# A hybrid trunk step: all eight gates of the attention's output branch computed among the independent linears

## The chip, the cores and the metric

The kernel runs on one core of a Trainium2 chip. The metric is the device time of one execution in microseconds (us); lower is better. TensorE (PE) multiplies, VectorE (DVE) and ScalarE (ACT) work elementwise, GpSimd (POOL) has little to do here, and SyncE (SP) issues nearly all DMA transfers, in the order of its queue.

## What is computed

A trunk of two layers works on 640 tokens of width 1024: 128 prompt tokens and 512 sample tokens. In each layer one wide projection feeds three branches, a gated short convolution, a bidirectional gated DeltaNet and an attention, and each branch has its own gate of 1024 columns:

```python
h = rms_norm(x, lp['g_pre1']) * (1 + sc1) + sh1
(cb, cc, cx, aq, ak, av, dn_q, dn_k, dn_v, dn_z, dn_beta, dn_a, gate_logits) = jnp.split(
    h @ lp['w_in'], SPLIT_IDX, axis=-1)
ya = (cb * depthwise_conv(cc * cx, lp['conv_w'])) @ lp['w_pa']
yb = block_attention(q, keys, vals) @ lp['w_pb']
yc = gated_deltanet_bidir(dn_q, dn_k, dn_v, dn_z, ...) @ lp['w_pc']
ga, gb, gc = jnp.split(jax.nn.sigmoid(gate_logits), 3, axis=-1)
mix = (ga * ya + gb * yb + gc * yc) @ lp['w_o']
x = x + gt1 * rms_norm(mix, lp['g_post1'])
h2 = rms_norm(x, lp['g_pre2']) * (1 + sc2) + sh2
ffn = (silu(h2 @ lp['w_gate']) * (h2 @ lp['w_up'])) @ lp['w_down']
```

The shifts, scales and gates of the modulation (`sh1`, `sc1`, `gt1` and so on) come from products of a conditioning vector with `w_mod`.

## The kernel before

Activations stand transposed, as eight tiles of 128 columns by 640 tokens, and are worked on in two halves of 320 tokens. Each fp32 product is made of three products in a shorter format: a tile is split into a high and a low part (ScalarE's cast `whi` at L94, VectorE's difference `wlo` at L95), and `mm3` multiplies high by high, high by low and low by high (L363 to L365). A **linear** is 128 output columns: 8 tiles of the contraction, two halves, three products, 48 matmuls, with two weight loads of 256 KB (`wraw`). The halves of a linear alternate by four tiles (12 matmuls), and each fills one of three PSUM banks (`NL` = 3, L72), so the second half of a linear can start only when the first half of the linear before it has been copied out.

The DeltaNet works on four heads in two pairs (`delta_pair`). For each head the projections k, q and v are computed and convolved (`dn_qkv`, `dn_post`, whose padded copy is `padc` at L861 and whose result is `dz`), turned over by TensorE (`nat`, L899), multiplied with themselves (`kk`, L946) and scaled by decays. The decays of a head are read back from DRAM, spread over the partitions (`rowb`, L905), and ScalarE exponentiates them first at L960 (`egl`). Then a triangular inverse of 32-wide blocks begins with VectorE's transposes `RA` and `RB` (L998) and TensorE's small products from L1018 on, followed by a scan over five chunks in both directions (`scan`, L1067 to L1079), whose start state `ss` comes from DRAM. The first head of a layer is special: its three projections are part of the group of linears that opens the layer (`lead`), so no linear is issued for them in `delta_pair` (the item is `None`). After both pairs come the keys and values and the attention's heads and stages (`attn_head`), with products `sco`, `psc`, transposes `ptT` (L770) and products with the values `po` (L780 to L782).

All these chains have waits in them. Beside them the kernel puts independent linears: `run(main, fill)` walks through the main chain, whose steps yield a cost in us, and after each step takes steps from the filler until the filler's costs have caught up:

```python
for c in main:
    tm += c * rate
    while fill is not None and tf < tm:
        ...
        tf += t
```

The costs are the constants `Y_*` at the head of the file: `Y_QKV` for a projection or its convolution, `Y_INV` for a step of the inverse (eight per pair, sixteen per layer), `Y_SCAN` for a step of the scan (five per pair, ten per layer). A gate linear yields 6.5. The filler of a layer is

```python
yield from branch(l, 0, ya, "w_pa", True)
yield from gates(l, 2)
yield from gates(l, 1, 0, NGB)
while len(yf) < 4:
    yield None
yield from weave(branch(l, 2, resplit(yf, "F"), "w_pc"), mods, PB)
```

preceded by the output gates of the DeltaNet (`dn_z`) and the convolution branch. `gates(l, b, m0, m1)` computes gate linears of branch b early and stores each result to DRAM (`sgd`, 320 KB); `branch(l, b, ...)` reads those back (`sgl`) and computes the rest at its own place. Branch 1, the attention's, runs after the attention, outside `run`. `mods` are the modulation products of layer 0 for later (`mod_part`, loads `wm` of 512 KB at L317, three buffers, products `pm` at L324): one step is taken per `PB` = 8 us of yields in branches 2 and 1, and the rest at once behind branch 1. In layer 1 there are none. The Tile framework then orders each engine's instructions by its own priorities within these limits.

Of the kernel before, what the change touches and what calls it, by code (L numbers as in the profile page):

```python
# [35 lines left out]
KEEP = ("C", "C", "C", "C", "E", None)  # L36
LEAD = ("C", "C", "C", "C", "E")
F1 = 14
NGB = 4
NPD = 2  # L40
NLD = 2

# [1 line left out]
NSQ = (2, 2, 2, 2, 2, 2, 2, 1)  # L44
ENDG = (3, 7)

Y_QKV, Y_NAT, Y_EL, Y_INV, Y_SCAN, Y_O = 1.127, 4.215, 1.207, 1.962, 2.959, 2.917
Y_AT, Y_AQ, Y_AK, Y_AKK, Y_DO = 0.446, 1.037, 0.438, 2.07, 2.558
PB, PF = 8.0, 11.5

# [2 lines left out]
def tile_trunk(ctx: ExitStack, tc: tile.TileContext, I: dict, O: list, layers=DEPTH):  # L53
# [340 lines left out]
    def linear(src, acts, ev):  # L394


        pb = {}
        i0 = 0
        for hi, lo, nk in wblocks(src, len(acts)):
            for h in range(2):  # L400
                if i0 == 0:
                    pb[h] = lbank()[:, :HF]
                for j in range(nk):
                    ah, al = acts[i0 + j]
                    mm3(pb[h], hi[:, j, :], lo[:, j, :], hv(ah, h), hv(al, h), i0 + j == 0, i0 + j == len(acts) - 1)
                if i0 + nk == len(acts):
                    ev(h, pb[h])
            i0 += nk
# [111 lines left out]
    def gates(l, b, m0=0, m1=KD):  # L520

        for m in range(m0, m1):
            SY.dma_start(out=sgd[b, m], in_=gate(l, b, m))
            gated.add((l, b, m))
            yield 6.5
# [339 lines left out]
    def dn_post(l, which, h, t):  # L865
        y = cslot("dy", (P, 641))
        ci = 92 + which * 4 + h
        conv3(y, t, lambda i: cols[l][:, ci + 12 * i:ci + 12 * i + 1])
        s = cslot("ds", (P, 641))
        A.activation(s, y, AF.Exp, scale=-1.0)  # L870
        sig_tail(s)
        z = cslot("dz")
        V.tensor_mul(z[:, 0:P], y[:, 0:P], s[:, 0:P])
        V.tensor_mul(z[:, P:NT], y[:, P + 1:641], s[:, P + 1:641])
        if which == 0:
            sq = cslot("dsq")
            A.activation(sq, z, AF.Square)

            def later():
                pr = bank("dqr")  # L880
                for c in range(5):
                    T.matmul(pr[:, 2 * c:2 * c + 2], lhsT=sq[:, c * P:(c + 1) * P], rhs=onesc, start=True, stop=True)
                r = rqs[l, h] = small("dqr", (P, 10), 4)
                rstd(r, pr[:, 0:10], 1.0, post=lnq)

            rqs[l, h] = later
        return z
# [20 lines left out]
    def delta_pair(l, hp, gz, out, first=None):  # L908
# [6 lines left out]
        for h in hs:  # L915
# [5 lines left out]
            for w, (item, t) in todo:  # L921
                if item is not None:
                    linear(*item[:3])
                    yield Y_QKV
                res[w] = dn_post(l, w, h, t)
                yield Y_QKV
            kT[h], qT[h] = res[1], res[0]
            Gbs = [rowb(l, 4 * d + h) for d in range(2)]
            kn[h] = nat(kT[h], f"kn{h}")
# [341 lines left out]
    for l in range(layers):  # L1271
# [7 lines left out]
        def mainc():  # L1279
            for hp in range(2):  # L1280
                yield from delta_pair(l, hp, gz, on, qkv if hp == 0 else None)
                for h in (2 * hp, 2 * hp + 1):
                    yf.append(dn_out(l, h, on[h], zs[h]))
                    yield Y_DO
            yield from attn_kv(l, kv)
            yield from attn_q(l, 0, kv, qs)
            pend = []
            for h in range(NH):
                stages, of = attn_head(l, h, kv, qs)
                for n, (fa, fb, pr2) in enumerate(stages):  # L1290
                    args = () if pr2 is None else (pr2,)
                    sm_ = fa(*args)
                    yield Y_AT
                    pend.append((fb, args, sm_))
                    if len(pend) > NPD:
                        f_, a_, s_ = pend.pop(0)
                        f_(*a_, s_)
                        yield Y_AT
                    if n == 0 and h + 1 < NH:
                        yield from attn_q(l, h + 1, kv, qs)  # L1300
                o.append(of)
            for f_, a_, s_ in pend:
                f_(*a_, s_)

        def fillc():
# [6 lines left out]
# [3 lines that stand above are left out]
# [98 lines left out]
```

## Time and profile before

| | us |
|---|---|
| median of 3 runs | 2776.02 |
| lowest and highest run | 2770.52, 2776.62 |
| the profiled execution | 2778.18 |
| its span in the trace | 2776.1 |

The profile is of one execution, 2.16 us above the median; 2.1 us of it lie outside the span. TensorE is busy 98% of the span, at a mean granted clock of 0.991 of full speed. A busy TensorE in these rows may be a matmul that is only queued in the pipeline, so the distance between the starts of matmuls, not the duration of one, tells what a matmul costs in a dense stretch. Layer 0 lies from about 30 to 1400 us and layer 1 from there on.

### The profile page before, as it was taken

What the parts mean: (1) busy time and instruction counts of PE and PEld (TensorE: products, weight loads), DVE (VectorE), ACT (ScalarE), POOL (GpSimd) and SP (SyncE); (2) the same over time, 40 slices, a digit from 0 to 9 for tenths busy, and PEclk for the clock granted to TensorE, in tenths of its full rate; (3) what the DMA queues carried; (4) which work ended last, traced back from release to release, by engine and by line L of the source; (5) the groups of instructions that cost most, each with busy time, mean ns of one, the idle gap of its engine ahead of it and who ended that gap; (6) DMA issues with size and microseconds to landing.
All of it is one profiled execution on the core that took longest, in us unless ns stands there. A gap on an engine that the chain in (4) does not pass through costs nothing.

```text
span 2776.1 us, 49612 instructions
## 1 busy us (share of the span) xinstructions
PE 2709.4 (98%) x19706; PEld 2583.2 (93%) x19706; DVE 1565.0 (56%) x3385; ACT 1256.8 (45%) x2863; POOL 26.5 (1%) x147
## 2 busy tenths in 40 slices
PE   7999999999999999999999999999999999999998
PEld 3899999999898999999978999999999999999997
DVE  4586576477743744224475865754777466442344
ACT  4533554466533633223455335545655354332333
POOL 0000000000000000000000000000000000000001
PEclk9999999999999999999999999999999999999999
DMA  8452355433564344444532323433233432222231
GB/s 240 72 80 48 80 94 112 83 66 96 161 163 154 123 130 152 125 158 145 170 89 58 73 52 82 96 90 85 68 95 117 125 99 88 76 69 76 81 117 62
DMA packets 387512, 288.15 MB, mean 104 GB/s; under 512 B 18667, under 2 KB 348113, under 8 KB 387281
## 3 DMA queue, kind: packets, MB, share of 16 engines
q1 hardware_dynamic: 387280, 285.00, 39.2%
q8 instruction: 154, 2.52, 0.4%
q14 instruction: 78, 0.63, 0.1%
HBM read 251.86 MB, written 33.07 MB: 103 GB/s over the span
## 4 chain that ended last, share of the span: by engine, by line
PE 84%; DVE 7%; DMA 5%; ACT 3%; issue 1%; SPq 0%; ACTq 0%; DVEq 0%
PE l L363 23%; PE l L364 23%; PE l L365 22%; DMA wm<-in_w_mod_dram 2%; PE pm L324 1%; DMA wraw<-in_w_in_dram 1%; PE ptT L770 1%; DMA rowb<-gd 1%; PE po L780 1%; PE scan L1071 1%; PE po L782 1%; PE kk L946 1%; PE sco L363 1%; PE po L781 1%; DVE Tt L990 1%
## 5 line engine op out<-in xcount | busy, mean ns | idle before, releaser
L94 ACT CAST whi<-wraw 128x512 fp32r<-128x512 f32 (+1 forms) x540 | 332.2, 616 | 829.4 <-PE l L364 783.7
L95 DVE TENSOR_TENSOR wlo<-wraw,whi 128x512 fp32r<-128x512 f32 (+1 forms) x540 | 367.4, 682 | 529.5 <-ACT whi L94 513.4
L363 PE MATMUL l<-hh,whi 128*128 128x320 f32 x1856 | 589.0, 317 | 2.8 <-ACT padc L861 2.8
L364 PE MATMUL l<-hl,whi 128*128 128x320 f32 x1856 | 582.7, 314 | 0.0
L365 PE MATMUL l<-hh,wlo 128*128 128x320 f32 x1856 | 581.7, 313 | 0.0
L363 PE MATMUL l<-h2h,whi 128*128 128x320 f32 x1248 | 387.4, 310 | 0.0
L364 PE MATMUL l<-h2l,whi 128*128 128x320 f32 x1248 | 385.3, 309 | 0.0
L365 PE MATMUL l<-h2h,wlo 128*128 128x320 f32 x1248 | 385.3, 309 | 0.0
L363 PEld LDWEIGHTS l<-hh,whi 128*128 128x128 f32 x1856 | 352.0, 190 | 6.5 <-ACT padc L861 3.3
L364 PEld LDWEIGHTS l<-hl,whi 128*128 128x128 f32 x1856 | 351.9, 190 | 2.0
L365 PEld LDWEIGHTS l<-hh,wlo 128*128 128x128 f32 x1856 | 352.1, 190 | 1.0
L363 PEld LDWEIGHTS l<-h2h,whi 128*128 128x128 f32 x1248 | 234.6, 188 | 7.0 <-ACT fs L427 3.1
L364 PEld LDWEIGHTS l<-h2l,whi 128*128 128x128 f32 x1248 | 234.6, 188 | 0.0
L365 PEld LDWEIGHTS l<-h2h,wlo 128*128 128x128 f32 x1248 | 234.6, 188 | 0.0
L363 PE MATMUL l<-ah,whi 128*128 128x320 f32 x544 | 168.8, 310 | 0.0
L364 PE MATMUL l<-al,whi 128*128 128x320 f32 x544 | 168.2, 309 | 0.0
L365 PE MATMUL l<-ah,wlo 128*128 128x320 f32 x544 | 167.9, 309 | 0.0
L363 PE MATMUL l<-rsh,whi 128*128 128x320 f32 x384 | 119.8, 315 | 0.0
L364 PE MATMUL l<-rsl,whi 128*128 128x320 f32 x384 | 118.4, 312 | 0.0
L365 PE MATMUL l<-rsh,wlo 128*128 128x320 f32 x384 | 118.2, 310 | 0.0
L363 PEld LDWEIGHTS l<-ah,whi 128*128 128x128 f32 x544 | 102.2, 188 | 2.2 <-issue 1.3
L365 PEld LDWEIGHTS l<-ah,wlo 128*128 128x128 f32 x544 | 102.2, 188 | 0.0
(427 smaller groups left out, 5328.2 us busy)
## 6 DMA issues: line engine op xcount, KB each, us to landing
wraw<-in_w_in_dram SPq DMA_DIRECT2D x256, 256.0 KB
wm<-in_w_mod_dram SPq DMA_DIRECT2D x80, 512.0 KB
wraw<-in_w_gate_dram SPq DMA_DIRECT2D x88, 256.0 KB
wraw<-in_w_up_dram SPq DMA_DIRECT2D x88, 256.0 KB
wraw<-in_w_down_dram SPq DMA_DIRECT2D x80, 256.0 KB
mixo<-mixd SPq DMA_DIRECT2D x32, 320.0 KB
wm<-in_w_mod_dram SPq DMA_DIRECT2D x32, 256.0 KB
wraw<-in_w_pb_dram SPq DMA_DIRECT2D x32, 256.0 KB
```

The source lines that it names most:

```text
L94: A.copy(hi, src)
L95: V.tensor_sub(lo, src, hi.bitcast(F32))
L324: T.matmul(pm[32 * u:32 * u + 2, 0:256], lhsT=sc[:, k, :], rhs=w[:, u * 256:(u + 1) * 256], start=(n == 0), stop=(n == KD - 1))
L363: T.matmul(out, lhsT=wh, rhs=ah, start=first, stop=False)
L364: T.matmul(out, lhsT=wh, rhs=al, start=False, stop=False)
L365: T.matmul(out, lhsT=wl, rhs=ah, start=False, stop=last)
L770: T.transpose(pt[:, i, q * P:(q + 1) * P], sm_[q][:, kt * P:(kt + 1) * P], ident)
L780: T.matmul(po, lhsT=vh, rhs=th, start=(kt == 0), stop=False)
L781: T.matmul(po, lhsT=vl, rhs=th, start=False, stop=False)
L782: T.matmul(po, lhsT=vh, rhs=tl, start=False, stop=(kt == 4))
L946: chunked("kk", lambda o, c: T.matmul(o, lhsT=kT[h][:, c * P:(c + 1) * P], rhs=rhs[:, c * P:(c + 1) * P], start=True, stop=True), lambda b ...
L990: V.tensor_add(Tt[:, j + 1:32, 0:j], Tt[:, j + 1:32, 0:j], tv)
```

## The change

`NGB` goes from 4 to 8: all eight gates of branch 1 are computed by the filler, stored and read back, and none is left behind the attention. The costs that the main chain yields grow: `Y_INV` from 1.962 to 2.6, `Y_SCAN` from 2.959 to 3.4, and the three convolution steps of the first head of each layer yield a new `Y_FIRST` of 3.5 instead of 1.127. So the filler gets further ahead at these places. No instruction of the linears is added or removed; per layer four gate results more are stored to DRAM and read back.

```diff
--- before.py
+++ after.py
@@ -36,7 +36,7 @@
 KEEP = ("C", "C", "C", "C", "E", None)
 LEAD = ("C", "C", "C", "C", "E")
 F1 = 14
-NGB = 4
+NGB = 8
 NPD = 2
 NLD = 2
 
@@ -44,7 +44,8 @@
 NSQ = (2, 2, 2, 2, 2, 2, 2, 1)
 ENDG = (3, 7)
 
-Y_QKV, Y_NAT, Y_EL, Y_INV, Y_SCAN, Y_O = 1.127, 4.215, 1.207, 1.962, 2.959, 2.917
+Y_QKV, Y_NAT, Y_EL, Y_INV, Y_SCAN, Y_O = 1.127, 4.215, 1.207, 2.6, 3.4, 2.917
+Y_FIRST = 3.5
 Y_AT, Y_AQ, Y_AK, Y_AKK, Y_DO = 0.446, 1.037, 0.438, 2.07, 2.558
 PB, PF = 8.0, 11.5
 
@@ -923,7 +924,7 @@
                     linear(*item[:3])
                     yield Y_QKV
                 res[w] = dn_post(l, w, h, t)
-                yield Y_QKV
+                yield Y_QKV if item is not None else Y_FIRST
             kT[h], qT[h] = res[1], res[0]
             Gbs = [rowb(l, 4 * d + h) for d in range(2)]
             kn[h] = nat(kT[h], f"kn{h}")
```

Line numbers from L49 on are one higher after the change. The change moves instructions as follows.

**First place: TensorE at the first head's products `kk` in layer 1.** `nat` and `kk` belong to the first head, the tiles `l_...` to linears beside them (`hh0` to `hh7` are the eight tiles of the contraction, so a linear's half runs from `hh0` to `hh7`). Before:

```order
L899 MATMUL nat_16237<-ident_64,dz_16219 128x128 x2
L899 MATMUL nat_16242<-ident_64,dz_16219 128x128 x2
L946 MATMUL kk_16333<-dz_16194 128x128 x3
L946 MATMUL kk_16338<-dz_16194 128x128 x2
L946 MATMUL kk_16342<-dz_16206,dz_16194 128x128 x3
L946 MATMUL kk_16347<-dz_16206,dz_16194 128x128 x2
L882 MATMUL dqr_16351<-onesc_67,dsq_16209 128x2 x5
L363 MATMUL l_16417<-hh4_15045,whi_16413 128x320
```

And now:

```order
L365 MATMUL l_16355<-hl7_15064,whi_16338 128x320
L366 MATMUL l_16355<-hh7_15063,wlo_16339 128x320
L947 MATMUL kk_16410<-dz_16206 128x128 x3
L947 MATMUL kk_16415<-dz_16206 128x128 x2
L947 MATMUL kk_16419<-dz_16218,dz_16206 128x128 x3
L947 MATMUL kk_16424<-dz_16218,dz_16206 128x128 x2
L883 MATMUL dqr_16428<-onesc_67,dsq_16221 128x2 x5
L364 MATMUL l_16497<-hh0_15049,whi_16487 128x320
```

Before, `kk` stood in the middle of the second head's first projection, between its tiles 3 and 4. Now the two `nat` rows stand further ahead (out of the piece), and `kk` stands between a finished linear and tile 0 of a linear of the convolution branch; that whole linear of 48 matmuls follows before the second head's next projection.

**Second place: ScalarE at the second head of layer 1.** `egl` waits for the decays, `padc` copies out the second head's projections, `whi` are casts of weights. Before:

```order
L447 COPY ccs_16404<-l_16430 128x320
L94 CAST whi_16565<-wraw_16563 128x512
L960 ACTIVATE egl_16927<-rowb_16784 128x5
L94 CAST whi_16641<-wraw_16639 128x512
L965 ACTIVATE Dt_16382<-Dt_16382 128x640
L861 COPY padc_16469<-l_16493 128x128
L861 COPY padc_16469<-l_16493 128x192
L960 ACTIVATE egl_16949<-rowb_16786 128x5
L94 CAST whi_16647<-wraw_16645 128x512
L861 COPY padc_16469<-l_16506 128x320
```

And now:

```order
L95 CAST whi_16644<-wraw_16642 128x512
L961 ACTIVATE egl_17004<-rowb_16866 128x5
L966 ACTIVATE Dt_16459<-Dt_16459 128x640
L95 CAST whi_16650<-wraw_16648 128x512
L961 ACTIVATE egl_17026<-rowb_16868 128x5
L95 CAST whi_16710<-wraw_16708 128x512
L862 COPY padc_16554<-l_16578 128x128
L862 COPY padc_16554<-l_16578 128x192
L95 CAST whi_16716<-wraw_16714 128x512
L862 COPY padc_16554<-l_16591 128x320
```

Before, the second `egl` stood between the copies of the first and the second half of the first projection; now both `egl` stand ahead of all copies, with one cast more between the last `egl` and the first copy.

**Third place: SyncE's queue at the end of layer 0's mixing, where the modulation loads `wm` stand among the loads of `w_o`.** Before:

```order
L359 DMA wraw<-in_w_o_dram 128x4x128
L490 DMA h2h_9880<-xd 128x640
L490 DMA h2h_9882<-xd 128x640
L490 DMA h2h_9884<-xd 128x640
L359 DMA wraw<-in_w_o_dram 128x4x128
L490 DMA h2h_9886<-xd 128x640
L317 DMA wm<-in_w_mod_dram 128x1024 x3
L359 DMA wraw<-in_w_o_dram 128x4x128
L317 DMA wm<-in_w_mod_dram 128x1024 x2
L359 DMA wraw<-in_w_o_dram 128x4x128 x5
```

And now:

```order
L360 DMA wraw<-in_w_pb_dram 128x4x128
L318 DMA wm<-in_w_mod_dram 128x1024 x2
L360 DMA wraw<-in_w_o_dram 128x4x128 x4
L318 DMA wm<-in_w_mod_dram 128x1024 x2
L360 DMA wraw<-in_w_o_dram 128x4x128 x2
L318 DMA wm<-in_w_mod_dram 128x1024 x2
L360 DMA wraw<-in_w_o_dram 128x4x128
L318 DMA wm<-in_w_mod_dram 128x1024 x7
L360 DMA wraw<-in_w_o_dram 128x4x128 x5
```

Before, the last five loads stood as three and two with the reload of `h2h` ahead of them. Now thirteen stand in this piece, seven of them in a row, and the `h2h` loads stand further ahead in the queue.

## Rows read from the trace of the kernel before

**Rows 1.** The page: the chain that ended last, shares of the span by engine.
```profile
PE 84%; DVE 7%; DMA 5%; ACT 3%; issue 1%; SPq 0%; ACTq 0%; DVEq 0%
```

**Rows 2.** The timeline of TensorE (start, duration, line, operation, tiles, idle before).
```profile
108.06 2.40 PE L946 MATMUL kk<-dz 128*128 128x128 f32 x20
...
1488.71 2.40 PE L946 MATMUL kk<-dz 128*128 128x128 f32 x20
...
1491.98 0.40 PE L363 MATMUL l<-hh,whi 128*128 128x320 f32 x1
...
1492.52 0.31 PE L363 MATMUL l<-hh,whi 128*128 128x320 f32 x1
...
1496.05 0.31 PE L363 MATMUL l<-hh,whi 128*128 128x320 f32 x1
...
1514.66 0.64 PE L363 MATMUL l<-hh,whi 128*128 128x320 f32 x1 [2.52 <-ACT padc L861]
```

**Rows 3.** Busy time by window: PE, PEld, DVE, ACT, POOL, granted clock, DMA, GB/s.
```profile
85.00:110.00 25.00, 21.63 (x155) 21.36 (x154) 12.13 (x20) 14.60 (x34) 0.00 (x0) 1.00 0.27 53
205.00:213.00 8.00, 6.72 (x70) 5.77 (x68) 5.78 (x10) 1.94 (x5) 0.42 (x1) 0.86 0.23 36
213.00:266.00 53.00, 53.00 (x539) 48.14 (x540) 35.66 (x86) 16.27 (x36) 0.00 (x0) 0.96 0.26 49
733.00:760.00 27.00, 23.65 (x192) 18.56 (x191) 20.09 (x55) 15.68 (x45) 0.00 (x0) 1.00 0.62 195
845.00:872.00 27.00, 24.22 (x201) 21.09 (x201) 5.61 (x11) 6.75 (x16) 0.00 (x0) 1.00 0.58 198
1480.00:1517.00 37.00, 32.90 (x222) 31.93 (x221) 23.61 (x50) 20.09 (x57) 1.77 (x16) 0.97 0.29 70
1588.00:1596.00 8.00, 6.76 (x67) 5.80 (x66) 5.70 (x10) 1.94 (x5) 0.42 (x1) 0.82 0.22 39
1844.00:1851.00 7.00, 7.00 (x70) 6.09 (x67) 3.82 (x8) 2.24 (x5) 0.00 (x0) 0.76 0.25 84
2119.00:2136.00 17.00, 14.23 (x95) 11.50 (x94) 13.78 (x41) 11.35 (x34) 0.00 (x0) 1.00 0.15 54
```

**Rows 4.** What TensorE waited for in 1480:1517 (total, times, longest us).
```profile
PE l L363 <- ACT padc L861: 2.8, 2, 2.5
PE nat L899 <- DVE dz L873: 1.3, 1, 1.3
```

**Rows 5.** The timeline of ScalarE in 1490:1516, second head of layer 1.
```profile
1506.82 0.21 ACT L960 ACTIVATE egl<-rowb 128x5 f32<-128x5 f32 x1 [2.04 <-DMA rowb<-gd]
...
1512.10 0.74 ACT L870 ACTIVATE ds<-dy 128x641 f32<-128x641 f32 x1 [3.71 <-DVE dy L566]
```

**Rows 6.** The timeline of ScalarE in 108:132, second head of layer 0.
```profile
124.98 0.21 ACT L960 ACTIVATE egl<-rowb 128x5 f32<-128x5 f32 x1 [3.32 <-DMA rowb<-gd]
...
125.60 0.48 ACT L861 COPY padc<-l 128x128 f32<-128x128 f32 x2
```

**Rows 7.** What TensorE waited for in 200:215, where the first inverse begins.
```profile
PE pw L1018 <- DVE RB L998: 1.3, 1, 1.3
```

**Rows 8.** What TensorE waited for in 470:476, the second pair's scan in layer 0.
```profile
PE scan L1067 <- DMA ss<-in_state_dn_dram: 0.9, 1, 0.9
```

**Rows 9.** What TensorE waited for in 2119:2136, the end of layer 1's attention.
```profile
PE po L780 <- ACT pTh L94: 1.2, 1, 1.2
PE psc L363 <- ACT p L725: 1.1, 1, 1.1
```

**Rows 10.** The timeline of TensorE in 845:872, the modulation products.
```profile
859.72 1.48 PE L324 MATMUL pm<-wm,sc 128*2 128x256 f32 x24 [1.81 <-DMA wm<-in_w_mod_dram]
...
866.48 1.04 PE L324 MATMUL pm<-wm,sc 128*2 128x256 f32 x16 [0.97 <-DMA wm<-in_w_mod_dram]
```

**Rows 11.** The timeline of SyncE's queue in 765:872, the modulation loads.
```profile
851.17 1.28 SPq L317 DMA_DIRECT2D wm<-in_w_mod_dram  x3
...
860.40 1.51 SPq L317 DMA_DIRECT2D wm<-in_w_mod_dram  x2
```

## The prediction

> **What bounds the kernel now.** I read the page first: TensorE holds 84% of the chain that ended last [rows 1], and the change takes no matmul away. So the time can only come from the places where TensorE waits or is clocked down, and the second view is busy time by window around them [rows 3]. The price of a linear comes from the timeline: from 1492.52 to 1496.05 there are 24 starts [rows 2], 0.147 us each, so a linear of 48 matmuls takes 7.05 us. The reader is to see four kinds of loss. In the first head of layer 1 TensorE idles 37 - 32.90 = 4.1 us in the window 1480:1517, and the waits there name ScalarE's `padc` (2.8) and VectorE's `dz` (1.3) [rows 3, 4]. At the start of the first pair's inverse it waits 1.3 us for `RB` [rows 7], and the granted clock is 0.86 in 205:213 and 0.96 in 213:266; layer 1 shows 0.82 at the same place [rows 3]. At the end of each attention it idles 3.35 us (733:760) and 2.77 us (2119:2136). At the end of layer 0's mixing it idles 2.78 us [rows 3], all for `wm` (1.81 and 0.97) [rows 10]. Inside the inverse (213:266) TensorE is busy throughout [rows 3], so a linear that is put there fills nothing.
>
> **The change, part by part.** Four more gates are 4 x 6.5 = 26 of filler cost per layer. Against them the spending grows by 3 x (3.5 - 1.127) = 7.1 at the first head, 16 x (2.6 - 1.962) = 10.2 at the inverse and 10 x (3.4 - 2.959) = 4.4 at the scan, 21.7 in all. The rest, 4.3 or 0.66 of a gate linear, is filler that reaches further into the attention. The matmuls are the same, so I sum up waits.
>
> First head of layer 1. Before, `kk` started at 1488.71 [rows 2]; the queue then held half a linear, a linear and 12 matmuls before the half that needs the bank of the first `padc` copy. That is 3.27 us (`kk` and the small products behind it, to 1491.98 [rows 2]) + 84 x 0.147 = 15.6 us after `kk`, while ScalarE stood at `egl` for `rowb`, the last time until 1506.82, and later until 1512.10 for `dy` [rows 5]. Now a whole linear stands where half a one did, and the need comes at 3.27 + 108 x 0.147 = 19.1 us. ScalarE, with its second `egl` at 18.1 us after `kk` if `rowb` lands as late, has a cast and two copies to go, until about 19.4: 0.3 us of wait are left. The next need, 7.05 later at 26.5, meets a copy that before let TensorE go on at 1514.66, 25.95 us after `kk` [rows 2]. Layer 0 already has this spacing: `kk` at 108.06, the last `egl` at 124.98 and the copy at 125.60, 17.5 us after `kk` [rows 2, 6], where no `padc` wait followed. So -2.8 + 0.3 = **-2.5**. The `dz` wait shrinks by the six matmuls that now stand ahead of it: 6 x 0.147 = **-0.9**. The clock of 0.97 over 37 us is 1.1 us of loss [rows 3]; I take half, **-0.5**, since the waits go but not the small products. Bounds for the three together: -5.2 (all goes) and +1.5 (`rowb` lands later behind more queue traffic).
>
> First head of layer 0: TensorE's 3.37 us in 85:110 are the wait for `dz` behind a blocked ScalarE, whose order is unchanged: **0**, bounds -1.5 and +1.5. Here 3.37 us of idling left the clock at 1.00 [rows 3]. The Trainium skill (TensorE: Matmul & The Clock Gate, Part 1: The HAM clock gate) says that the throttled rate is the default and activity releases it; by that rule alone every wait taken away would return clock too, about another -1 here. The row does not agree, and the sum stays by the row.
>
> Start of the inverse, both layers: seven linears lie between the second `kk` and `RB` before and after, and VectorE's work there is the same list, so `RB` comes as late: **0**. Bounds: -1.3 and -3.2 each (0.14 x 8 + 0.04 x 53 for the clock), +1. Second pair: a clock of 0.76 over 7 us in 1844:1851 [rows 3] is 1.7 us, of which more linears among the small products may return half: **-0.8** (0 to -1.7). Layer 0's scan waits 0.9 us for `ss` [rows 8]; three linears more stand ahead of it, **-0.6** (0 to -0.9).
>
> Ends of the attention. In layer 1, by the order, the filler ended with about 1.3 heads of the attention still to come, and the waits are short ones for `p` and `pTh` [rows 9]; the order now puts linears among them to the end: of 2.77, **-2.5** (0 to -2.8). In layer 0 linears of branch 2 already stood there, and of 3.35 part is `wm`: **-1.2** (+1 to -3).
>
> End of layer 0's mixing. Branch 1 now yields 51.2 us of cost instead of 77.2, so at one step per 8 us 6 of the modulation steps are taken there instead of 9. Counted in TensorE's order, the last groups of products are 12, 12 and 8 as before, but two groups of 8 that stood among branch linears stand now directly ahead of them. A round of three loads went from 851.17 to 860.40, 9.2 us; a round of two from there to the end of its products at 866.48 + 1.04, 7.1 us [rows 10, 11]. Rounds of 2, 3, 3, 2 are 32.6 us; between them lie 2.46 linears (17.3) and 5.0 of products. So up to 10.3, less about 1 by which the same count for the two rounds of before exceeds its 2.8, is exposed: +6.5 over before at most, 0 if the third buffer keeps one load ahead each time. I take **+3.5**. The stores and reloads of four gates more per layer cost nothing in TensorE's time as long as they land before their linear; DMA share is 0.58 to 0.62 in the windows of layer 0 where they fall [rows 3], and if that cover went, it would show as the same kind of wait.
>
> Sum: -2.5 - 0.9 - 0.5 - 0.8 - 0.6 - 2.5 - 1.2 + 3.5 = -5.5. Against the profiled execution 2778.18 gives 2772.7; it stands 2.2 above the median, so the median should go from 2776.02 to **2770.5**.
>
> **The rivals.**
> *Nothing comes out.* The `rowb` landing decides ScalarE, and more DMA traffic could move it by the 3.5 us that the linear wins; then the first head keeps its 3.9, and the attention's 3.7 pays for the modulation's 3.5. Left: -0.8 - 0.6 - 0.2 = -1.6, 2774.4. For it: ScalarE's order keeps both `egl` ahead, now even ahead of all copies. Against: layer 0 [rows 6]. A form of it, that the change does not do what it says, is ruled out by the order: 3.6 instead of 3.3 linears stand inside layer 0's first inverse, 3.5 instead of 2.7 inside the second.
> *Slower: the modulation loads block `w_o`.* Seven `wm` stand in a row in SyncE's queue with `w_o`'s loads behind them. If the rounds are fully exposed (+6.5) and the next weights then land a round late (8.5 us, 851.17 to 859.72), the sum is -5.5 - 3.5 + 6.5 + 8.5 = +6.0, 2782. It decides once the last `wm` is issued later than 1.2 linears (8.5 us) before TensorE reaches the weights behind it; the order gives 1.6 linears, which speaks against it.
> *Faster: the clock holds at the inverse.* If denser linears end the drop at both first inverses early, -6.4 more, 2764. Against: both waits for `RB` stay. The skill's rule that activity releases the throttle (same page and part) is for it; rows 3 show the drop only beside the short products, not at every wait.
>
> **How the numbers follow.** A difference of 0.2%, 5.5 us, is about what a measurement of this kernel can tell from none. Forecast 0.42, with a range of its own of 2765 to 2776 (0.24 faster, 0.17 same, 0.01 slower, as it sits on the mark); nothing 0.32 (0.05, 0.24, 0.03); blocked loads 0.14 (0, 0.02, 0.12); clock 0.12 (all faster). Together faster 0.41, same 0.43, slower 0.16. The range reaches to the rivals at either side, a little past the clock's: 2762 to 2782, with 0.1 left out on each side.
>
> **What would show it.** Right: in layer 1's second head no `padc` wait over 1 us; the wait for `RB` and the clock at 205:213 and 1588:1596 as before; linears up to the end of layer 1's attention with under 0.5 us idle; and `wm` waits of 4 to 8 us at the end of layer 0's mixing. Wrong: `wm` waits over 10 us or a wait for `w_o` weights, `padc` still waiting over 2 us, or a granted clock near 1.00 at the inverse.

## The result, and the profile after

| | median us | runs | lowest, highest us |
|---|---|---|---|
| before | 2773.66 | 4 | 2770.52, 2776.62 |
| after the change | 2799.81 | 4 | 2797.39, 2802.66 |

The change makes the kernel slower: ratio 1.0099, 95% interval 1.0087 to 1.0111, or 26 us. The forecast was 2770.5 with a range of 2762 to 2782, so the result lies outside the range and on the other side.

The page of the profiled execution of the changed kernel (span, busy times, chain):

```profile
span 2800.6 us, 49644 instructions
...
PE 2716.9 (97%) x19706; PEld 2588.8 (92%) x19706; DVE 1571.8 (56%) x3385; ACT 1258.7 (45%) x2863; POOL 26.5 (1%) x147
...
PE 78%; DVE 11%; DMA 5%; ACT 3%; issue 2%; SPq 0%; DVEq 0%; ACTq 0%
```

The count of matmuls is the same, 19706. TensorE's share of the chain fell from 84% [rows 1] to 78%, and VectorE's rose from 7% to 11%: the time went into waits behind other engines. What TensorE waited for over the whole span (total, times, longest us), among the rows that grew or are new:

```profile
PE pm L325 <- DMA wm<-in_w_mod_dram: 8.1, 3, 4.6
...
PE pw L1019 <- ACT Wp L1021: 4.6, 2, 2.8
PE l L364 <- DVE sgl L443: 4.6, 2, 4.4
...
PE l L364 <- ACT padc L862: 3.8, 2, 2.5
PE pw L1019 <- DVE RB L999: 3.1, 2, 1.9
```

Waits alone don't show the clock. So I counted lost time: for each pair of neighbouring instruction shapes on TensorE the lower quartile of the start-to-start distances, over all traces compared, is what that step costs at its best, and what a trace has above it is lost. The best costs sum to the same number in both kernels within 0.2 us (2545.2 and 2545.0), so the whole difference is lost time: 221.1 us before and 245.4 after, 24.3 more. A trace is one execution, and that of before, 2778.18, stands 4.5 us above the median of the table, so the differences to it come out low. Stages in which TensorE's order is the same differ by up to 5 us from trace to trace (layer 1's second pair: +7.0 in the change, +12.0 in f3 below), so one stage alone is read with that care. By stage, in us:

| stage | layer 0 before | after | layer 1 before | after |
|---|---|---|---|---|
| first head and first pair, to its scan | 19.9 | -1.8 | 18.5 | -4.0 |
| its scan, second pair, to the attention's first product | 18.7 | +9.3 | 18.9 | +7.0 |
| attention and mixing | 27.9 | +5.6 | 27.8 (with the feed-forward) | +3.8 |
| opening of the kernel, or from layer 0's mixing to layer 1's first head | 36.6 | +1.4 | 41.6 | +2.7 |

The columns "after" give the difference; the 11.2 us lost in the kernel's last stage grow by 0.3. The gain in the first head is there. The loss has two places: the second pair of heads in each layer (16.3 us) and the end of the attention (9.4 us). In the same count, 7.8 of the 16.3 lie between the start of the second pair's inverse and its scan (3.6 and 4.2), 5.5 between the pair's first `kk` and the inverse (4.0 and 1.5, the `padc` waits of 2.5 and 1.4 among them), and 2.8 ahead of that `kk`. The windows of the changed kernel (columns as in rows 3):

```profile
214.00:222.00 8.00, 6.80 (x75) 6.04 (x74) 7.87 (x16) 1.23 (x4) 0.42 (x1) 1.00 0.23 40
...
456.00:466.00 10.00, 8.19 (x76) 7.31 (x76) 2.31 (x6) 3.62 (x7) 0.00 (x0) 0.66 0.42 117
766.00:800.00 34.00, 28.39 (x205) 21.96 (x204) 22.88 (x54) 16.95 (x44) 0.00 (x0) 0.89 0.48 162
860.00:890.00 30.00, 26.54 (x215) 22.38 (x214) 7.13 (x13) 7.34 (x17) 0.00 (x0) 0.94 0.61 193
1500.00:1537.00 37.00, 35.98 (x254) 35.38 (x253) 26.60 (x56) 20.36 (x56) 1.78 (x16) 1.00 0.41 83
...
1848.00:1858.00 10.00, 7.17 (x79) 6.17 (x77) 1.97 (x5) 3.00 (x6) 0.00 (x0) 0.80 0.49 155
2165.00:2185.00 20.00, 15.49 (x111) 14.18 (x110) 16.73 (x38) 12.84 (x32) 0.00 (x0) 0.92 0.26 73
```

Layer 1's first head (1500:1537) idles 1.0 us at full clock where it idled 4.1 us at 0.97 [rows 3]. The second pair's inverse begins at 454.3 and 1847.7: there TensorE idles 1.8 and 2.8 us, and the clock stands at 0.66 and 0.80. The same place before, 436:446, was busy throughout at full clock:

```profile
436.00:446.00 10.00, 10.00 (x118) 8.78 (x116) 4.63 (x11) 4.12 (x9) 0.00 (x0) 1.00 0.82 119
```

What stands behind the wait in layer 1 is read from three queues at once. VectorE of the changed kernel (start, duration, line, operation, tiles, idle before):

```profile
1837.83 1.12 DVE L999 STREAM_TRANSPOSE RA<-Tt 128x512 f32<-128x512 f32 x1
...
1839.24 1.12 DVE L999 STREAM_TRANSPOSE RA<-Tt 128x512 f32<-128x512 f32 x1
1840.20 2.23 DVE L999 STREAM_TRANSPOSE RB<-Tt 128x512 f32<-128x512 f32 x2
...
1843.09 1.28 DVE L96 TENSOR_TENSOR wlo<-wraw,whi 128x512 fp32r<-128x512 f32 x2
1844.79 0.69 DVE L96 TENSOR_TENSOR wlo<-wraw,whi 128x512 fp32r<-128x512 f32 x1 [0.41 <-ACT whi L95]
1851.58 0.69 DVE L96 TENSOR_TENSOR wlo<-wraw,whi 128x512 fp32r<-128x512 f32 x1 [6.10 <-ACT whi L95]
```

SyncE's queue of the changed kernel, the loads of weights and what stands between them:

```profile
1842.50 0.34 SPq L616 DMA_DIRECT2D rope<-in_rope_dram  x1
1843.81 0.97 SPq L360 DMA_DIRECT2D wraw<-in_w_in_dram  x2
1844.83 0.49 SPq L524 DMA_DIRECT2D sgd<-sg  x1
1845.51 7.16 SPq L360 DMA_DIRECT2D wraw<-in_w_in_dram  x2
```

ScalarE of the changed kernel:

```profile
1850.93 0.62 ACT L95 CAST whi<-wraw 128x512 fp32r<-128x512 f32 x1 [4.45 <-DMA wraw<-in_w_in_dram]
1851.46 0.43 ACT L428 ACTIVATE sg<-l 128x320 f32<-128x320 f32 x1
1851.91 0.28 ACT L1021 COPY Wp<-pw 32x160 f32<-32x160 f32 x1
```

The reader is to see a chain. There are three buffers for raw weights, and `wlo` on VectorE frees one. While VectorE runs the transposes of the inverse, from 1837.8 to 1842.4, no `wlo` runs, so no load is issued; the loads come in a bunch from 1843.81 on, and the cast that needs one waits 4.45 us for it. On ScalarE the copy `Wp`, which the inverse needs, stands behind that cast. TensorE waits 2.8 us for `Wp`, and what follows runs at a lowered clock. Layer 0 shows the same at 456 (3.43 us for the weights, 1.8 for `Wp`). In the kernel before, one `wlo` ran between the transposes, and the cast ahead of `Wp` came in time. VectorE of before, layer 0:

```profile
424.49 1.14 DVE L998 STREAM_TRANSPOSE RA<-Tt 128x512 f32<-128x512 f32 x1
425.47 0.68 DVE L95 TENSOR_TENSOR wlo<-wraw,whi 128x512 fp32r<-128x512 f32 x1
426.08 2.26 DVE L998 STREAM_TRANSPOSE RB<-Tt 128x512 f32<-128x512 f32 x2
```

The load also takes long. By the turn of the three buffers, the cast at 1850.93 reads what was issued at 1843.81, 7.1 us before, and in between the DMA engines are 0.58 busy, so they are not full:

```profile
1843.80:1850.90 7.10, 5.61 (x45) 5.12 (x43) 1.27 (x2) 1.06 (x2) 0.00 (x0) 1.00 0.58 166
```

### The profile page after: what moved, and what is told of

The parts are those of the page before. It is cut to its first block, busy times and chain, and to the rows that moved or that the text cites. A ratio compares the mean times of both kernels' runs of the same rounds, so it can differ in the third digit from the quotient of the medians.

```text
span 2800.6 us, 49644 instructions
## 1 busy us (share of the span) xinstructions
PE 2716.9 (97%) x19706; PEld 2588.8 (92%) x19706; DVE 1571.8 (56%) x3385; ACT 1258.7 (45%) x2863; POOL 26.5 (1%) x147
## 4 chain that ended last, share of the span: by engine, by line
PE 78%; DVE 11%; DMA 5%; ACT 3%; issue 2%; SPq 0%; DVEq 0%; ACTq 0%
PE l L364 21%; PE l L365 21%; PE l L366 21%; DMA wraw<-in_w_in_dram 2%; PE pm L325 1%; DMA rowb<-gd 1%; DVE Tt L991 1%; DVE tmpE L989 1%; DVE wlo L96 1%; DMA wm<-in_w_mod_dram 1%; PE ptT L771 1%; PE po L781 1%; PE po L783 1%; PE sco L364 1%; PE scan L1072 1%
## 5 line engine op out<-in xcount | busy, mean ns | idle before, releaser
L365 PEld LDWEIGHTS l<-al,whi 128*128 128x128 f32 x544 | 102.2, 188 | 0.0
```

What stands on the lines that cost most here:

```text
L365: T.matmul(out, lhsT=wh, rhs=al, start=False, stop=False)
```

## The experiments

All ratios are to the kernel before, run on the same chip beside it. "Second pair" and "attention's end" are the stages of the table above, as differences to before in lost time, layer 0 and layer 1.

| run | ratio, 95% interval | second pair | attention's end |
|---|---|---|---|
| the change | 1.0099 (1.0087 to 1.0111) | +9.3, +7.0 | +5.6, +3.8 |
| e1 rope on POOL's queue | 1.0098 (1.0083 to 1.0113) | +11.3, +10.0 | +3.2, +3.4 |
| e2 eight gates, old costs | 1.0050 (1.0035 to 1.0065) | +0.7, -1.1 | +8.4, +5.9 |
| e3 four gates, new costs | 1.0224 (1.0208 to 1.0239) | +14.4, +17.2 | +10.9, +10.9 |
| e4 first head alone | 1.0097 (1.0080 to 1.0114) | +11.4, +5.1 | +7.5, +5.1 |
| e7 inverse and scan alone | 1.0093 (1.0076 to 1.0110) | +11.3, +2.0 | +8.7, +8.4 |
| e5 fourth weight buffer | 1.0050 (1.0035 to 1.0065) | +6.3, +2.8 | +0.2, +5.0 |
| b5 the same in before | 1.0052 (1.0037 to 1.0066) | +4.4, +0.3 | +1.7, +4.2 |
| e6 Wp on VectorE | 1.0078 (1.0063 to 1.0093) | +5.9, +5.8 | +2.2, +1.3 |
| f1 Y_EL 1.27 | 1.0035 (1.0022 to 1.0048) | +9.1, +5.7 | -0.2, -0.8 |
| f2 Y_EL 1.27 in before | 1.0074 (1.0057 to 1.0091) | +8.3, +0.5 | +5.0, +7.9 |
| f3 PB 5.3 | 1.0089 (1.0074 to 1.0104) | +9.0, +12.0 | +2.3, +0.8 |
| e8 Y_AT 0.52 | 1.0070 (1.0055 to 1.0085) | +7.9, +8.8 | +0.3, +0.1 |
| g2 repairs, Y_SCAN 3.2 | 1.0059 (1.0047 to 1.0072) | +5.0, +4.1 | +2.6, +4.7 |
| g1 repairs, Y_SCAN 2.959 | 1.0000 (0.9992 to 1.0009) | +4.3, +2.4 | -3.6, +0.1 |
| e9 rowb on POOL's queue | 1.0112 (1.0091 to 1.0134) | +9.9, +7.1 | +3.0, +0.8 |
| h1 g1 with the scan's cost split | 1.0004 (0.9995 to 1.0013) | +2.5, +3.1 | -3.7, 0.0 |

**Which part of the change costs.** First the parts alone.

```diff
 e2: before with     NGB = 8
 e3: the change with NGB = 4
 e4: the change with Y_INV, Y_SCAN = 1.962, 2.959
 e7: the change with Y_FIRST = 1.127
```

> The kernel before with eight early gates and the old costs: the linears beside DeltaNet stand as before, and the four gates more reach into the attention's end. Theory A: the second pair shows no wait for Wp and no low clock; the end of the attention and the mixing behind it lose 8 to 14 us; ratio 1.003 to 1.005. If the loss came from the four gates' stores and reloads themselves, the ratio would stay at 1.010.

> The changed kernel with four early gates (NGB = 4): the new costs alone. The order of TensorE up to the attention is that of the changed kernel. Theory A: the second pair loses its 13 to 14 us as in the changed kernel, and the end of the attention loses nothing or up to 4 us (the filler ends earlier); ratio 1.004 to 1.006. If the loss came from the number of early gates, the ratio would be 1.000.

> The changed kernel with the old costs of the inverse and the scan: eight gates, spent at the first head alone. Between the second pair's last kk and its inverse stand 7.5 linears (7 in the changed kernel, 8 before). Theory A: about half the second pair's loss is left (5 to 8 us), the first head of layer 1 keeps its gain of 3 us, and the attention's end loses 10 us or more; ratio 1.004 to 1.007. Rival B: no difference to the changed kernel in the second pair.

> The changed kernel with Y_FIRST = 1.127 as before: eight gates, spent at the inverse and the scan alone. Between the second pair's last kk and the inverse stand 7.5 linears. If the first head's spending is what puts the second pair out of step, the second pair costs under 3 us in each layer and the ratio is 1.005 or less; if it is the tighter spacing of 7 or 7.5 instead of 8 linears, the second pair loses 5 us or more in each layer and the ratio is 1.007 to 1.010.

Eight gates with the old costs leave the second pair as it was (TensorE's order is that of before up to 620 us, and again in layer 1's two pairs) and lose at the attention's end, as expected. The new costs alone bring the second pair's loss, and their ratio is far worse than expected (1.0224): with 21.7 more of spending and no more filler the independent linears run out before the scan and the attention, so the stage that ends at the attention's first product loses 14.4 and 17.2 us, and the attention's end 10.9 in each layer. So in the change the gates pay for the costs; neither half is good alone. Spending at the first head alone and at the inverse and the scan alone both bring layer 0's loss of 11 us, and both expectations fell in part: it isn't one of the two sums that does it. In layer 1, e7 loses only 2.0 and e4 5.1. What e3, e4 and e7 have in common with the change is only that the linears stand elsewhere against DeltaNet's own work.

**Why the second pair waits.** The first theory put the blame on SyncE's queue, where `rope` waits for `RB` ahead of the weights.

```diff
-        SY.dma_start(out=rt, in_=I["rope"])
+        G.dma_start(out=rt, in_=I["rope"])
```

> The changed kernel with one transfer moved: the load of the rotary table (rope) is issued by POOL's queue instead of SyncE's. Theory A (SyncE's queue: in the second pair rope waits there until RB is done and the next gate linear's weights stand behind it; their cast then blocks ScalarE ahead of the copy Wp that the inverse waits for): the waits for Wp of 1.8 and 2.8 us go, and with them most of the low clock behind them, together 8 to 11 us; ratio to the kernel before about 1.006 instead of 1.010. Rival B (VectorE is the bound and RB itself is late) and rival C (the weights are late because the DMA engines are full): within 2 us of the change, 1.009 to 1.010.

The theory fell: 1.0098. With `rope` gone from the queue, the weights still were issued only once VectorE had done the transposes. ScalarE of this run, layer 0, shows both waits:

```profile
447.49 0.62 ACT L95 CAST whi<-wraw 128x512 fp32r<-128x512 f32 x1 [2.96 <-DVE RB L999]
...
455.06 0.62 ACT L95 CAST whi<-wraw 128x512 fp32r<-128x512 f32 x1 [3.50 <-DMA wraw<-in_w_in_dram]
```

So the next theory was the buffer: a load waits for a `wlo`, and VectorE has none among its transposes.

```diff
-NH_, NC_, NF_, NT_ = 16, 24, 16, 4
-NWR, NW = 3, 4
+NH_, NC_, NF_, NT_ = 16, 24, 16, 3
+NWR, NW = 4, 4
```

> The changed kernel with four buffers for raw weights (wraw) instead of three, paid for with one temporary (tag T, 4 to 3); TensorE's order is that of the changed kernel. Theory A2 (the weights come late because a load waits for the buffer that wlo on VectorE frees, and VectorE runs the inverse's transposes without a wlo among them): the 3.5 and 4.4 us that ScalarE's cast waits for weights at the second inverse go, with the waits for Wp and the low clock behind them: 8 to 12 us less than the changed kernel, ratio to before 1.005 to 1.007. Rival D (the weights are there, and ScalarE's order alone or the switching of linears and small products costs the time): 1.009 to 1.010.

> The same two numbers (wraw 4, T 3) in the kernel before: the control. Theory A2: weights are late there only in the layer openings, at most 3 us gained, ratio 0.999 to 1.000; if it gains as much as the changed kernel does (8 us or more, 0.997), the buffer is a general bound and not the cost of this change.

With a fourth buffer the second pair's inverse begins without a wait in the changed kernel. ScalarE of e5 in layer 1, and the window of its inverse:

```profile
1836.15 0.62 ACT L95 CAST whi<-wraw 128x512 fp32r<-128x512 f32 x1 [1.17 <-PE l L365]
1836.68 0.43 ACT L428 ACTIVATE sg<-l 128x320 f32<-128x320 f32 x1
1837.13 0.28 ACT L1021 COPY Wp<-pw 32x160 f32<-32x160 f32 x1
```

```profile
1836.00:1846.00 10.00, 10.00 (x114) 8.88 (x114) 2.67 (x6) 4.36 (x9) 0.00 (x0) 1.00 0.62 175
```

The cast waits for no weight any more, `Wp` follows it at once, and the clock stays at 1.00. From the inverse to the scan the lost time is 0.9 and 1.6 us below before, where the change was 3.6 and 4.2 above; nothing was done to the order. The ratio, 1.0050, is what the theory expected, but not by the inverse alone: of the 16.5 us less lost time than in the change's trace 7.2 lie in the second pairs (where the `padc` waits ahead of the inverse stay), 5.4 at layer 0's attention's end, and 4.9 in the kernel's opening, where the control gains 4.0 as well. The control went against its expectation: the same two numbers make the kernel before slower by 0.5%. There the second pair's inverse hardly changes (+0.1 and -1.6 from the inverse to the scan), but 4.4 us are lost between layer 0's scan and the attention and 4.2 at layer 1's end. So the buffer that comes free late is the cause of this wait in the change, and a fourth is not a way to a faster kernel; whether the loss comes from the fourth buffer or from the temporary that paid for it is open, since I didn't part the two.

Then the order on ScalarE alone:

```diff
-                    A.copy(Wp[qb], pw[qb, :, 0:32])
+                    V.tensor_copy(Wp[qb], pw[qb, :, 0:32])
```

> The changed kernel with the inverse's copy Wp on VectorE instead of ScalarE. Theory D (Wp is late only because it stands behind a cast that waits): the waits of 1.8 and 2.8 us for Wp go and with them some low clock, 5 to 10 us less than the changed kernel, ratio 1.006 to 1.008. Theory A2 (the linear beside it needs the late weights anyway): the wait moves to that linear's weights, and the ratio stays within 0.1% of the changed kernel's, 1.009 to 1.010.

1.0078, inside the range of theory D, but not by its mechanism. The wait stayed and moved to VectorE: in 1835:1860 of this run TensorE waits for `Wp` there, behind a `wlo` that waits for the same late weights. TensorE's order also differs from the change's from the first inverse on, and from the second inverse to the scan this run loses only 2.1 and 1.2 us less than the change, so the ratio says little about `Wp` alone.

```profile
PE pw L1025 <- DVE Wp L1021: 3.1, 1, 3.1
```

**Whether the spacing does it.** In the change seven linears stand between the second pair's last `kk` and its inverse, before it were eight.

```diff
-Y_EL = 1.207
+Y_EL = 1.27
```

> The changed kernel with the elimination's cost Y_EL raised from 1.207 to 1.27: eight linears instead of seven stand between a pair's last kk and its inverse, in both pairs, and the filler's costs are then spent in full, so that the attention's linears stand as before (four later). Theory S (spacing: with seven linears VectorE's elimination and transposes end too late for both the weights of the next linear and RB): in both pairs the wait for RB, the wait for Wp and the low clock behind them go; 12 to 18 us less than the changed kernel in DeltaNet, and 4 to 8 less at the attention's end; ratio to before 0.998 to 1.003. Rival F (the filler at the inverse and the scans, more linears among the small products, is what costs): the loss stays, 1.006 or more.

> The kernel before with Y_EL = 1.27 and nothing else: eight linears in the first pair too (seven before), eight in the second as before. Theory S: the first pair's waits for RB of 1.3 us and the low clock behind them (3 us) go in both layers, and the earlier end of the filler costs 1 to 3 us at the attention's end; ratio 0.996 to 0.999. Rival F: no change or slower, 1.000 to 1.003.

In the changed kernel (f1) eight linears stand ahead of all four inverses, and the waits for `RB` and `Wp` are gone but for 0.2 us; 1.0035 is a little above what was expected. Windows of the second pairs' inverses in f1:

```profile
454.00:464.00 10.00, 10.00 (x121) 8.67 (x120) 4.21 (x9) 4.19 (x9) 0.00 (x0) 1.00 0.45 91
1840.00:1850.00 10.00, 10.00 (x120) 8.79 (x117) 4.56 (x10) 4.48 (x9) 0.00 (x0) 1.00 0.42 122
```

What is left of its loss stands in large part behind a new wait: by then, it seems, the filler has run dry, and the first products of the keys and values (`vn`) wait 5.9 and 3.2 us for a PSUM bank behind VectorE's `yc`. But f2 refutes the spacing as a rule: the kernel before with eight linears in every place is slower by 0.7%. Its waits for `RB` are gone as well, and yet layer 0's second pair waits 3.3 us for `Wp`. ScalarE of f2:

```profile
437.93 0.62 ACT L94 CAST whi<-wraw 128x512 fp32r<-128x512 f32 x1 [2.47 <-DMA wraw<-in_w_in_dram]
...
442.76 0.62 ACT L94 CAST whi<-wraw 128x512 fp32r<-128x512 f32 x1 [3.87 <-DMA wraw<-in_w_in_dram]
...
443.74 0.28 ACT L1020 COPY Wp<-pw 32x160 f32<-32x160 f32 x1
```

The transposes were done some 11 us ahead of that inverse, and the casts still are late. Here the transfers themselves are slow: the DMA engines are full over 432:439 and move 100 GB/s, where the change's late load had them 0.58 busy at 166:

```profile
432.00:439.00 7.00, 7.00 (x49) 6.84 (x47) 1.11 (x2) 3.40 (x6) 0.00 (x0) 1.00 1.01 100
```

So e1's rival C, weights late because the DMA engines are full, fits f2 and not the change's layer 1; why the engines move so little there is open. A load can be late because its buffer comes free late or because its transfer is slow. In these traces TensorE waits where such a late cast stands in ScalarE's queue ahead of `Wp`. e5 takes the lateness of the change's second inverse away and that part of the loss with it; the number of linears alone does not decide.

**The end of the attention.** Two edits of the changed kernel:

```diff
 e8:  Y_AT 0.446 -> 0.52
 f3:  PB 8.0 -> 5.3
```

> The changed kernel with the attention's cost Y_AT raised from 0.446 to 0.52: the filler's last linears stand ahead of the attention's last steps instead of being cut through by them; DeltaNet as in the changed kernel. If layer 1's wait of 4.6 us for a PSUM bank behind the splits of the attention's output comes from linears that reach to the very end, layer 1 loses 4 us less at the end and layer 0 1 to 3 less; ratio 1.007 to 1.008. If not, 1.009 to 1.010.

> The changed kernel with PB = 5.3 instead of 8.0: one modulation step per 5.3 us of cost in branches 2 and 1, nine steps in branch 1 as before the change. If the modulation loads are what layer 0 loses at the attention's end and the mixing behind it (waits for wm of 5.0, 0.7 and 2.9 us), 4 to 7 us of its loss go and layer 1 stays; ratio 1.007 to 1.008. If not, 1.009 to 1.010.

With the filler spent a little ahead of the attention's last steps (e8) the end of the attention loses 0.3 and 0.1 us against before instead of 5.6 and 3.8, and 1.0070 is at the better end of what was expected. In layer 1 of the change the last linears of branch 2 wait 4.4 us for a PSUM bank: VectorE had the splits `rsl` of the attention's output (3.0 us in a row at 2177.88) ahead of the step that empties the bank (L443). VectorE, then TensorE:

```profile
2177.88 3.04 DVE L96 TENSOR_TENSOR rsl<-o,rsh 128x640 fp32r<-128x640 f32 x4 [0.34 <-ACT rsh L95]
...
2183.51 0.89 DVE L443 TENSOR_TENSOR sgl<-sgl,l 128x320 f32<-128x320 f32 x2
2184.05 0.64 PE L364 MATMUL l<-rsh,whi 128*128 128x320 f32 x1 [4.42 <-DVE sgl L443]
```

In e8 that wait is gone. Taking modulation steps more often (f3) takes 3.3 us from layer 0's end, less than the 4 to 7 expected, but its second pair in layer 1 loses 5 us more in that trace, with TensorE's order there unchanged, and the ratio of 1.0089 can't be told from the change. So the modulation's part, about 3 us, is measured by its stage alone and not shown by the ratio.

**The wait ahead of the second pair.** In the change TensorE waits 2.5 us (layer 0) and 1.4 (layer 1) for `padc` at the second pair's first head.

```diff
-        SY.dma_start(out=t, in_=gd[l][:, dh, :].partition_broadcast(P))
+        G.dma_start(out=t, in_=gd[l][:, dh, :].partition_broadcast(P))
```

> The changed kernel with the decay rows rowb loaded by POOL's queue instead of SyncE's. If the padc waits at the second pair's first head (2.6 us in layer 0, 1.6 in layer 1) come from rowb standing in SyncE's queue behind a store and weight loads, they go, 4 to 6 us less than the changed kernel, ratio 1.007 to 1.008; if the transfer itself is slow or the data late, 1.009 to 1.010.

This run doesn't tell: POOL's own queue had other work ahead, and the second load was issued at 365.14, 10.1 us behind the pair's first `kk`, no earlier than SyncE had issued it in the change (9.6 us behind). It landed 10 us later:

```profile
365.14 0.87 POOL L906 DMA_DIRECT2D rowb<-gd  x1 [0.31 <-issue]
```

The ratio is 1.0112, and TensorE waits 2.6 us there still, now for `sg` behind the same `egl`. The other candidate was a missing linear, tried together with all repairs:

```diff
 g2: the change with Y_EL 1.27, Y_SCAN 3.2,   Y_AT 0.50, PB 5.3
 g1: the change with Y_EL 1.27, Y_SCAN 2.959, Y_AT 0.52, PB 5.3
 h1: as g1, but
-            yield Y_SCAN
+            yield (3.4,2.6)[hp]
```

> All repairs in one: the changed kernel with Y_EL = 1.27 (eight linears ahead of each inverse), Y_SCAN = 3.2 (filler left for the step from the scan to the attention, where the kernel with Y_EL alone waited 5.9 and 3.2 us for yc), Y_AT = 0.50 (no filler at the attention's very end) and PB = 5.3 (modulation steps as densely as before). The waits found so far are then gone, and the first pair's RB wait with them: DeltaNet 4 to 8 us faster than before, the attention's end within 2 us of before; ratio 0.996 to 0.999. If the losses only move to other places, 1.000 to 1.005.

> As the other repair, but Y_SCAN = 2.959 as before and Y_AT = 0.52. Its order puts the second pair's first nat at 30.5 to 31.5 linears as in the changed kernel (31.0 to 31.5 in the kernel with Y_EL alone), where the changed kernel waited 2.6 us for padc. If that position is what brings the padc wait, this one loses 3 to 4 us against the other repair in layer 0; if not, the two agree within 2 us. Ratio 0.997 to 1.001.

> The repair with Y_SCAN = 2.959 (g1), with the scan's cost split between the pairs: 3.4 in the first, 2.6 in the second. In g1's order ScalarE's two egl stand directly ahead of the padc copies at the second pair's first heads, and TensorE waits 2.8 and 2.0 us there; here one gate linear stands between (its sg rows lie around the second egl), as in the kernel with Y_EL alone, where no such wait was. If the padc wait comes from that missing linear, 4 us go in layer 0 and 3 in layer 1: ratio 0.997 to 0.998, faster than both kernels. If it comes from the rowb transfer itself, the ratio stays at 1.000.

g1 is level with the kernel before, 1.0000 (0.9992 to 1.0009): the repairs together give back as much as the change lost. It is a balance: its second pairs still lose 6.7 us against before, and the first pairs and layer 0's attention gain. Its profiled execution has 4.9 us less lost time than the one of before, about as much as the latter stood above the median. g2 fell short (1.0059, outside both of its expectations): it has waits of 2.8 us for `p` in the middle of both attentions, which g1 hasn't. At the second pair's first head it waits 2.9 and 2.2 us for `sg` behind the same `egl`, about as long as g1 for `padc`, so the position of `nat` was the wrong mark. h1 shows what brings the wait: there the first half of a gate linear is copied out (`sg`) between the two `egl` steps and the second half behind them, ahead of the `padc` copies, and TensorE has no wait in 345:375, although ScalarE still waits about as long for `rowb` (8.7 us in the change):

```profile
ACT egl L961 <- DMA rowb<-gd: 8.0, 2, 5.6
```

In g2 a gate linear stands there too, but both its halves are copied out behind the second `egl`, and there TensorE waits. So at this place half a linear decides.

From the second pair's first `kk` to its inverse, h1 loses 1.2 us in layer 0, as before (1.3), where g1 loses 5.6. The ratio stays at 1.0004, because the stages around it lose more: TensorE waits 1.9 us for a cast ahead of `onT` in layer 1, for one. No version that I ran is faster than the kernel before.

## Why the prediction was wrong

- **First head of layer 1**: right. -3.9 was expected; the stages of the first head and up to the inverse lose 0.7 and 2.8 us less (3.5), and in 1500:1537 no `padc` wait is left.
- **First pairs' inverse, both layers**: as forecast, the waits for `RB` stay (3.1 us in two, 2.5 before). The clock was to stay low, and near 1.00 was a sign of being wrong: it is 1.00 at layer 0's first inverse (214:222) and 0.88 at layer 1's. The 2.5 us that layer 0 gains there lie inside the bounds, but they are luck, and not shown to come from the change: see the clock below.
- **The second pair is the step that failed.** The prediction priced it by two small gains, -0.8 for the clock and -0.6 for `ss`, and held that a linear inside the inverse "fills nothing", so costs nothing. It measured +16.3 in the two layers together. Of that, 7.8 are the late weights ahead of `Wp` with the clock behind them, which e5 takes away, and 5.5 lie between the first `kk` and the inverse, where h1 takes layer 0's part away. The order showed eight linears before the second inverse and seven now; the prediction made that comparison for the first pair and not for the second. f2, with eight, waits as well, so the count was only a hint that the inverse meets other weights. "Fills nothing" is true only as long as the linear's weights are there: a linear brings two casts and two splits that stand in the queues of the engines the inverse needs.
- **The `padc` wait** that the change was to take from layer 1's first head (2.8 us) went from there and came back at the second pair's first head in both layers (2.5 and 1.4). The prediction had the landing of `rowb` as a risk for the first head only.
- **Ends of the attention**: -2.5 and -1.2 with +3.5 for the modulation. The waits for `wm` grew from 4.8 us to 8.1, 3.3 as forecast, but the largest, 4.6, stands at the attention's end and not in the mixing. The two gains have the wrong sign: the stages lose 5.6 us in layer 0, 3.3 of it `wm`, and 3.8 in layer 1. Linears that reach to the last step cover TensorE only until their results have to go through VectorE just as it splits the attention's output, and e8 shows that this loss can be avoided.
- **The rivals.** The slower one (weights of `w_o` blocked by `wm`) did not happen: the waits for the output projection's linears in 880:935 (3.0 us for `y`) are no longer than before (3.6). So most of the 0.16 for a slower kernel went to a cause that wasn't there, and what did happen, weights and decays late in ScalarE's queue in front of a chain step, was not among the rivals.
- **The clock.** By the rows, an idle of 3.4 us left the clock at 1.00 in one place [rows 3]; in the change's layer 0, TensorE idles 1.8 us in 456:458 at 0.98, and then the clock is at 0.50, the lower of its two levels, through the inverse's short products:

```profile
456.00:458.00 2.00, 0.19 (x4) 0.16 (x4) 0.69 (x1) 1.42 (x4) 0.00 (x0) 0.98 0.94 258
458.00:464.00 6.00, 6.00 (x63) 5.15 (x62) 1.13 (x4) 1.57 (x3) 0.00 (x0) 0.50 0.38 106
```

  The Trainium skill (TensorE: Matmul & The Clock Gate, Part 1: The HAM clock gate) has the engine's activity release the throttle; a fall behind idling agrees with that, but it does not price a wait. e2 has TensorE's order of the kernel before there and nearly the same wait for `RB`, 1.2 us (1.3 before), yet its clock stays at 1.00 where rows 3 have 0.86:

```profile
203.80:211.80 8.00, 6.80 (x75) 5.92 (x73) 6.31 (x12) 1.94 (x5) 0.42 (x1) 1.00 0.24 37
```

  From the inverse to the scan e2 loses 2.9 us less than before in both layers. So the drops that the prediction priced from its one trace (-3.2 for each first inverse in the bounds and in the rival on the clock) differ between executions of one order, and are no fixed cost that the change could give back or keep.

## What to carry to other kernels

When filler work is moved, follow its whole train, not its matmuls alone: the load that needs a free buffer, the cast and the split that stand in the in-order queues of the engines which the critical chain also uses. A wait showed up where the last of these stood ahead of a step of the chain, so look at three queues at the same moment (the loads, the caster, the engine that frees the buffer), and compare the order at every place where the chain recurs, not at the first alone. And test a tuned cost table as a whole: here one half of the change alone cost 0.5%, the other 2.2%, both together 1.0%, and the edits that repaired one place opened waits of 2 to 6 us at the next.

## What the runs showed that I had not expected

A weight load of 256 KB came 4.45 us late for its cast although the DMA engines were 0.58 busy from its issue on (1843.80:1850.90); with one buffer more the wait was gone. In f2 the same kind of load was late with the engines full (432:439) at 100 GB/s, so the two look alike on ScalarE and differ in the DMA share. One buffer more took 0.5% from the changed kernel and put 0.5% on the kernel before (2788.61 against 2773.97). And taking `rope` out of SyncE's queue gave nothing: the weight loads were not held up by its place there.
